# Norm statistics turned around: squares as the loaded operand, a token per partition, broadcast with the unit matrix

## The chip, the cores and the metric

The kernel runs on one core of a Trainium2 chip. The metric is the device time of one execution in microseconds; lower is better. All arithmetic of the norms is float32.

## The reference

One inference step of a small diffusion backbone with two layers (width D = 1024). Two token sets go through the same weights: 128 context tokens and 512 latent tokens. Layer 0 mixes tokens with a bidirectional state-space scan (four groups of 512 channels), layer 1 with differential attention (8 heads of 128 channels); each is followed by a gated convolutional FFN with 2816 hidden channels. What matters here are the root mean square norms:

```python
def _rms(x):
    xf = x.astype(F32)
    return xf * lax.rsqrt(jnp.mean(xf * xf, axis=-1, keepdims=True) + EPS)

y = _rms(y.reshape(b, l, SSD_GROUPS, SSD_INNER // SSD_GROUPS))   # per scan group, 512 channels
o = (_rms(o) * subln_g * (1.0 - lam_init))                       # per attention head, 128 channels
h = rmsnorm(x, g) * (1 + scale) + shift                          # before every mixer and FFN, 1024 channels
```

There are four norms over the model width inside the layers, one per scan group, one per attention head, and a final one over the model width.

## The kernel before

**Layout.** Activations lie transposed: channels on the 128 partitions, tokens along the free axis. The 512 latent tokens come first, then the 128 context tokens, 640 columns in all (`T`). A tensor of 1024 channels is 8 tiles of 128x640. The dense matmuls split weights and activations into a high and a low part of a reduced float32 format and make three products; each product is issued in two pieces, 256 columns (half A) and 384 columns (half B). For the last norm the tokens are cut the other way, 384 (half C) and 256 (half D). Weights stream in on SyncE's DMA queue, are rounded by ScalarE (`whi`) and VectorE (`wlo`), and are used once.

**A norm** sums over channels, so over partitions, which is done by matmul. `rms_bcast` (line 180) does it for all norms:

- `ms`: a 128x32 block of ones is the loaded operand (`lhsT`), the squares are streamed. The tokens are cut in four equal parts of n = 64, 96 or 160 columns; part j goes to the output partitions 32j to 32j+31. So the sums lie on a [128, n] tile, each of them 32 times over. If there are several tiles of squares (four for the norms inside and behind the layers: three of single channel tiles and one with the sum of five; eight for the very first norm), they accumulate in PSUM.
- `rsqrt` (line 165): an integer first guess and two refinements on VectorE, nine operations on [128, n] (tiles `rs_v`, `rs_a`, `rs_y`).
- The generator then yields, which lets other work be issued for `wait` steps.
- broadcast: a column of `sel` (0.375 at one of the partitions 0, 32, 64, 96, zero elsewhere), repeated to 128 columns, is the loaded operand, and `rs_y` is streamed. Each of four matmuls gives n columns, the same in all partitions. The tiles are called `nbc` (norms over the width), `gbc` (scan groups) and `obc` (heads). The factor 0.375 belongs to the last refinement.

Then VectorE multiplies the activations by the broadcast (`nt`, `xf`, `o`, `yt`).

`rms_bcast` runs 21 times: once for the first norm (all 640 tokens, eight tiles of squares, line 433), four times for the scan groups (640 tokens, one tile, line 832), eight times for the heads (640 tokens, one tile, line 1070), three times each for halves A and B of the norms between the sub-layers, and once each for C and D of the final norm (`norm_stats`, line 223).

**Order of the work.** The side work (scan, attention core, norms, modulation) is written as Python generators, kept in a list of tasks. Every dense k step calls `hook` (line 75), which counts a tick and advances the tasks whose wait is over; a task that yields w is taken up again w ticks later. One k step of a whole dense tile is six matmuls (three products, two halves); in the split last projections (`project_last`) and first tiles (`start_tiles`) it is three or six. From the program order a scheduler of the framework makes the queues of the engines; in the trace, for example, matmuls of a dense tile stand between those of one `ms`. Each engine works through its queue in order. Buffers that are reused (the PSUM tiles `d`, three in number, and `m` and `y`, one each, among others) are waited for.

Places where a norm's result is needed soon: after `project_last` the statistics of half A are computed while the last tiles' half B is still multiplied, and those of half B while the next sub-layer's first tiles (`st`) multiply half A. In `first_tiles` (line 366) the statistics stand ahead of the modulation rows (`modrow`), whose inputs (`mp`) come in by DMA into buffers that they free. At the end of the kernel, the statistics of half D, the root, the broadcast and the output tiles `yt` come after the last matmul of the last projection.

Of the kernel before, what the change touches and what calls it, by code (L numbers as in the profile page):

```python
# [18 lines left out]
P = 128  # L19
# [26 lines left out]
class Step:  # L46
# [118 lines left out]
    def rsqrt(self, y, ms, n, count):  # L165

        tile_ = lambda nm: self.pc.tile([P, 160], F32, tag=nm, name=nm, bufs=1)[:, :n]
        v, a = tile_("rs_v"), tile_("rs_a")
        V = self.nc.vector
        V.tensor_scalar(v, ms, 1.0 / count, EPS, ALU.mult, ALU.add)  # L170
        V.tensor_scalar(y.bitcast(I32), v.bitcast(I32), -0.5, RSQRT_MAGIC, ALU.mult, ALU.add)
        self.stt(a, y, -0.5, y, ALU.mult, ALU.mult)
        self.tt(a, a, v, ALU.mult)
        self.stt(y, a, 1.5, y, ALU.add, ALU.mult)
        self.tt(a, v, y, ALU.mult)
        self.tt(a, a, y, ALU.mult)
        self.stt(a, a, -10.0 / 3, a, ALU.add, ALU.mult)
        self.stt(y, a, 5.0, y, ALU.add, ALU.mult)

    def rms_bcast(self, alloc, sq, t0, t1, count, wait=4):  # L180


        n = (t1 - t0) // 4
        ms = self.bank("m", "ms")
        for i, s in enumerate(sq):
            for j in range(4):
                self.mm(ms[32 * j:32 * j + 32, :n], self.ones, s[:, t0 + j * n:t0 + (j + 1) * n],
                        i == 0, i == len(sq) - 1)
        y = self.pc.tile([P, 160], F32, tag="rs_y", name="rs_y", bufs=2)[:, :n]
# [3 lines left out]
        for j in range(4):  # L193
            self.mm(bc[:, j * n:(j + 1) * n], self.sel[:, j:j + 1].to_broadcast([P, P]), y, True, True)
        return bc

    def wide(self, name):

        return self.dense_ps(name)[:, 192:192 + T]
# [23 lines left out]
    def norm_stats(self, half):  # L223

        tag = {"A": "y", "B": "m", "C": "y", "D": "m"}[half]
        return self.rms_bcast(lambda: self.bank(tag, "nbc"), self.nsq, *HALF[half], D, 3)
# [78 lines left out]
    def load_consts(self):  # L305
        nc, a = self.nc, self.a
        self.ident, self.U, self.L = (self.cst[:, i * P:(i + 1) * P] for i in range(3))
        self.ones = self.cst[:, 3 * P:3 * P + 32]
        self.sel = self.cst[:, 3 * P + 32:3 * P + 36]
# [56 lines left out]
    def first_tiles(self, h, pool):  # L366
# [6 lines left out]
        self.cst = self.ct([P, 3 * P + 36], "cst")  # L373
# [656 lines left out]
    def att_tail(self, hd, w, ws, vs, os_, pool):  # L1030
# [39 lines left out]
        bc = yield from self.rms_bcast(lambda: self.wide("obc"), [sq], 0, T, P, 4 if hd == 7 else 7)  # L1070
# [114 lines left out]
def _consts():  # L1185
# [5 lines left out]
    cst = np.concatenate([I, U, L, np.ones((P, 32), f), f(0.375) * I[:, ::32]], axis=1)  # L1191
# [85 lines left out]
```

## Time and profile before

| | us |
|---|---|
| median of 3 runs | 1921.22 |
| lowest, highest | 1920.97, 1921.40 |
| the profiled execution | 1921.78 |
| its span, first to last instruction | 1920.0 |
| busy in it: TensorE, VectorE, ScalarE | 1887.8, 1377.3, 944.5 |

How to read the profile's lines. PE is TensorE's matmul, PEld its weight load (it overlaps PE), DVE is VectorE, ACT ScalarE, SP SyncE's DMA queue. In a timeline, a line gives the start in us from the start of the span, the duration in us, the engine, the line of the code, the operation and `out<-in` by tile names; "128*32 128x160 f32" is a matmul with 128 rows and 32 columns of the array in use and 128 partitions x 160 columns streamed. "x8" at the end are eight such instructions merged; in brackets stands the idle time before and what ended it. A matmul's duration includes its way through the array, so consecutive ones overlap: the distance between their starts, not the duration, is what one costs. In a view of one tile, three numbers with slashes are the least, median and greatest duration in ns, then come the first and last start. In the table by stretches each engine has its busy us and its count, and the last three columns are the granted TensorE clock, the DMA engines' share and GB/s. A line of the waits has the us in total, how often, and the longest.

### The profile page before, as it was taken

Reading aid. Unit: us, or ns where it says so; the run is one execution under the profiler, and the core shown is the slowest. Engines: PE = TensorE matmul, PEld = TensorE weight load, DVE = VectorE, ACT = ScalarE, POOL = GpSimd, SP = SyncE. Lnnn points to the kernel's source line nnn. Section 1 sums busy time; section 2 is a strip of 40 time slices with the busy share of each in tenths; the row PEclk is TensorE's granted clock in tenths of the full one; section 3 lists DMA queues with packets and bytes.
Section 4 is the critical chain, followed back from the end, with each engine's and each line's share of the span. In section 5 each row is a group of like instructions: output and inputs, shape, how many; then the busy total and the mean of one; then the engine's idle time right before and its main releaser. Section 6 shows DMA issues by size and latency. Waiting matters only on the chain.

```text
span 1920.0 us, 33586 instructions
## 1 busy us (share of the span) xinstructions
PE 1887.8 (98%) x13741; PEld 1781.4 (93%) x13741; DVE 1377.3 (72%) x2649; ACT 944.5 (49%) x1753; POOL 0.2 (0%) x4
## 2 busy tenths in 40 slices
PE   7999999999999999999999999999999999999997
PEld 4899898989989999999999989888899999999997
DVE  4779998989847999994455877788677553553554
ACT  3468585858525542343343566666446432441441
POOL 0000000000000000000000000000000000000000
PEclk9999999999999999999999999999999999999998
DMA  9612112123452556642222211111032222222211
GB/s 341 230 56 67 56 55 78 45 67 101 158 173 78 181 181 206 208 138 75 77 68 76 86 38 50 49 46 34 13 121 80 77 77 78 65 68 88 72 40 55
DMA packets 66730, 185.01 MB, mean 96 GB/s; under 512 B 8336, under 2 KB 14736, under 8 KB 66448
## 3 DMA queue, kind: packets, MB, share of 16 engines
q1 hardware_dynamic: 66000, 182.34, 29.3%
q8 instruction: 108, 1.77, 0.4%
q10 hardware_dynamic: 576, 0.52, 0.1%
q14 instruction: 46, 0.38, 0.1%
HBM read 177.06 MB, written 5.77 MB: 95 GB/s over the span
## 4 chain that ended last, share of the span: by engine, by line
PE 94%; DVE 2%; DMA 1%; ACT 1%; issue 0%; SPq 0%; DVEq 0%; ACTq 0%
PE up L103 30%; PE po L103 25%; PE z L103 6%; PE x L103 5%; PE st L103 5%; PE bc L103 3%; PE yp L103 3%; PE v L103 3%; PE q L103 2%; PE sl L103 2%; PE k L103 2%; PE ov L103 1%; PE modrow L103 1%; PE r L103 1%; PE wt L1052 1%; PE in L103 1%
## 5 line engine op out<-in xcount | busy, mean ns | idle before, releaser
L94 ACT ACTIVATE whi<-raw 128x1024 fp32r<-128x1024 f32 (+4 forms) x230 | 236.0, 1027 | 414.4 <-PE po L103 243.7
L100 DVE TENSOR_TENSOR wlo<-raw,whi 128x1024 fp32r<-128x1024 f32 (+4 forms) x230 | 270.3, 1177 | 183.8 <-ACT whi L94 178.1
L97 DVE SCALAR_TENSOR_TENSOR xr<-po,mod,xr 128x256 f32<-128x256 f32 (+2 forms) x231 | 89.0, 434 | 159.0 <-PE po L103 158.8
L103 PE MATMUL po<-mh,whi 128*128 128x256 f32 (+1 forms) x704 | 167.5, 310 | 0.0
L103 PE MATMUL po<-ml,whi 128*128 128x256 f32 (+1 forms) x704 | 167.2, 309 | 0.0
L103 PE MATMUL po<-mh,wlo 128*128 128x256 f32 (+1 forms) x704 | 167.0, 309 | 0.0
L103 PE MATMUL up<-h01h,wlo 128*128 128x256 f32 (+1 forms) x656 | 149.4, 308 | 0.0
L103 PE MATMUL up<-h11h,wlo 128*128 128x256 f32 (+1 forms) x656 | 149.4, 308 | 0.0
L103 PE MATMUL up<-h01h,whi 128*128 128x256 f32 (+1 forms) x656 | 149.3, 308 | 0.0
L103 PE MATMUL up<-h11h,whi 128*128 128x256 f32 (+1 forms) x656 | 149.3, 308 | 0.0
L103 PE MATMUL up<-h01l,whi 128*128 128x256 f32 (+1 forms) x656 | 149.3, 308 | 0.0
L103 PE MATMUL up<-h11l,whi 128*128 128x256 f32 (+1 forms) x656 | 149.3, 308 | 0.0
L103 PEld LDWEIGHTS po<-mh,whi 128*128 128x128 f32 x704 | 128.3, 188 | 0.6 <-ACT mh L94 0.4
L103 PEld LDWEIGHTS po<-mh,wlo 128*128 128x128 f32 x704 | 128.6, 188 | 0.0
L103 PEld LDWEIGHTS po<-ml,whi 128*128 128x128 f32 x704 | 128.4, 188 | 0.0
L103 PEld LDWEIGHTS up<-h01h,wlo 128*128 128x128 f32 x656 | 119.3, 188 | 0.0
L103 PEld LDWEIGHTS up<-h11h,wlo 128*128 128x128 f32 x656 | 119.3, 188 | 0.0
L103 PEld LDWEIGHTS up<-h11h,whi 128*128 128x128 f32 x656 | 119.3, 188 | 0.0
L103 PEld LDWEIGHTS up<-h01h,whi 128*128 128x128 f32 x656 | 119.3, 188 | 0.0
L103 PEld LDWEIGHTS up<-h01l,whi 128*128 128x128 f32 x656 | 119.3, 188 | 0.0
L103 PEld LDWEIGHTS up<-h11l,whi 128*128 128x128 f32 x656 | 119.2, 188 | 0.0
L97 DVE SCALAR_TENSOR_TENSOR ca<-uraw,fcw,ca 128x511 f32<-128x511 f32 (+1 forms) x176 | 85.2, 546 | 11.7 <-ACT ca L94 11.7
(505 smaller groups left out, 4469.2 us busy)
## 6 DMA issues: line engine op xcount, KB each, us to landing
raw<-in_w_up SPq DMA_DIRECT2D x88, 512.0 KB, 3.5
mw<-in_modT SPq DMA_DIRECT2D x48, 512.0 KB, 3.6
raw<-in_w_in SPq DMA_DIRECT2D x40, 512.0 KB, 3.5
raw<-in_w_dn SPq DMA_DIRECT2D x32, 448.0 KB, 3.3
raw<-in_w_qkv SPq DMA_DIRECT2D x24, 512.0 KB, 3.5
mr<-in_mod SPq DMA_DIRECT2D x44, 256.0 KB, 5.4
raw<-in_w_so SPq DMA_DIRECT2D x16, 512.0 KB, 4.1
raw<-in_w_dn SPq DMA_DIRECT2D x16, 512.0 KB, 3.7
```

What stands on the lines that cost most here:

```text
L94: return self.nc.scalar.activation(out, in_, func, **k)
L97: return self.nc.vector.scalar_tensor_tensor(out, in0, s, in1, op0, op1)
L100: return self.nc.vector.tensor_tensor(out, a, b, op)
L103: return self.nc.tensor.matmul(out, lhsT, rhs, start=start, stop=stop)
L1052: nc.tensor.transpose(pm[:, b * P:(b + 1) * P], ws[b][:, kc * P:(kc + 1) * P], self.ident)
```

## The change

The roles of the operands in the statistics are exchanged. Each 128 tokens of a tile of squares (128 channels x 128 tokens) become the loaded operand, and one column of ones is streamed. The sum of a token lands on the token's own partition, in column j for the j-th 128 tokens, so `ms` is [128, 2], [128, 3] or [128, 5] instead of [128, 64], [128, 96] or [128, 160]. The first matmul of a norm alone has the start flag, the last alone the stop flag. The root runs on these few columns and has a tenth operation, the multiplication by 3/8 that was in the selectors before. The broadcast loads column j of the root, repeated to 128 columns, and streams the unit matrix: the result has in every partition the roots of 128 tokens, and there is one such matmul for every 128 tokens. The waits between the statistics and the broadcast are shorter: 3 ticks instead of 4 as a rule, 2 instead of 3 for halves A to D, 5 instead of 7 for the heads (3 instead of 4 for the last head). The wide broadcast tile begins at column 128 of its two PSUM banks instead of 192, so that no chunk of 128 crosses a bank. The constants lose 31 columns of ones and the four selectors.

```diff
     def rsqrt(self, y, ms, n, count):
-        tile_ = lambda nm: self.pc.tile([P, 160], F32, tag=nm, name=nm, bufs=1)[:, :n]
+        tile_ = lambda nm: self.pc.tile([P, NCH], F32, tag=nm, name=nm, bufs=1)[:, :n]
...
         self.stt(y, a, 5.0, y, ALU.add, ALU.mult)
+        V.tensor_scalar(y, y, 3.0 / 8, None, ALU.mult)
...
-    def rms_bcast(self, alloc, sq, t0, t1, count, wait=4):
-        n = (t1 - t0) // 4
+    def rms_bcast(self, alloc, sq, t0, t1, count, wait=3):
+        n = (t1 - t0) // P
         ms = self.bank("m", "ms")
         for i, s in enumerate(sq):
-            for j in range(4):
-                self.mm(ms[32 * j:32 * j + 32, :n], self.ones, s[:, t0 + j * n:t0 + (j + 1) * n],
-                        i == 0, i == len(sq) - 1)
-        y = self.pc.tile([P, 160], F32, tag="rs_y", name="rs_y", bufs=2)[:, :n]
+            for j in range(n):
+                self.mm(ms[:, j:j + 1], s[:, t0 + j * P:t0 + (j + 1) * P], self.ones, i + j == 0, i + j == len(sq) + n - 2)
+        y = self.pc.tile([P, NCH], F32, tag="rs_y", name="rs_y", bufs=2)[:, :n]
         self.rsqrt(y, ms[:, :n], n, count)
         yield wait
         bc = alloc()
-        for j in range(4):
-            self.mm(bc[:, j * n:(j + 1) * n], self.sel[:, j:j + 1].to_broadcast([P, P]), y, True, True)
+        for j in range(n):
+            self.mm(bc[:, j * P:(j + 1) * P], y[:, j:j + 1].to_broadcast([P, P]), self.ident, True, True)
         return bc
     def wide(self, name):
-        return self.dense_ps(name)[:, 192:192 + T]
+        return self.dense_ps(name)[:, P:P + T]
...
-        return self.rms_bcast(lambda: self.bank(tag, "nbc"), self.nsq, *HALF[half], D, 3)
+        return self.rms_bcast(lambda: self.bank(tag, "nbc"), self.nsq, *HALF[half], D, 2)
...
-        self.ones = self.cst[:, 3 * P:3 * P + 32]
-        self.sel = self.cst[:, 3 * P + 32:3 * P + 36]
+        self.ones = self.cst[:, 3 * P:3 * P + 1]
...
-        self.cst = self.ct([P, 3 * P + 36], "cst")
+        self.cst = self.ct([P, 3 * P + 1], "cst")
...
-        bc = yield from self.rms_bcast(lambda: self.wide("obc"), [sq], 0, T, P, 4 if hd == 7 else 7)
+        bc = yield from self.rms_bcast(lambda: self.wide("obc"), [sq], 0, T, P, 3 if hd == 7 else 5)
...
-    cst = np.concatenate([I, U, L, np.ones((P, 32), f), f(0.375) * I[:, ::32]], axis=1)
+    cst = np.concatenate([I, U, L, np.ones((P, 1), f)], axis=1)
```

## The prediction

> **What bounds the kernel now.** I read the page first, then the waits, then the order of time around each norm. The page's head and its PE lines, and the line of the chain that ended last:
>
> ```profile
> span 1920.0 us, 33586 instructions
> ...
> PE 1887.8 (98%) x13741; PEld 1781.4 (93%) x13741; DVE 1377.3 (72%) x2649; ACT 944.5 (49%) x1753; POOL 0.2 (0%) x4
> ...
> PE 94%; DVE 2%; DMA 1%; ACT 1%; issue 0%; SPq 0%; DVEq 0%; ACTq 0%
> ...
> raw<-in_w_in SPq DMA_DIRECT2D x40, 512.0 KB, 3.5
> ```
>
> TensorE sets the end (the last line, a transfer's size and time to landing, is for the start). The table by stretches says the same of four attention heads, where VectorE and ScalarE have room:
>
> ```profile
> 1176.00:1322.00 146.00, 146.00 (x1026) 131.31 (x1028) 114.24 (x228) 89.76 (x190) 0.00 (x0) 1.00 0.15 46
> ```
>
> So a microsecond added to PE's queue between some 50 and 1903 us is a microsecond of the end, and one taken from VectorE there is worth next to nothing. The change is therefore a question of PE slots: what the statistics and the broadcast take of PE now, and after.
>
> **What one load costs.** The program has two PE instructions, each with its own weight load, for one float32 matmul (8 where the code asks for 4). The loads of the broadcasts, in the order of time: eight that stream 64 columns, eight that stream 96 and the load behind them; then their row in the view of one tile (ns, least/median/most):
>
> ```profile
> 585.32 0.97 PEld L103 LDWEIGHTS nbc<-rs_y,cst 128*128 128x128 f32 x8 [0.24 <-DVE rs_y L97]
> ...
> 601.91 0.97 PEld L103 LDWEIGHTS nbc<-rs_y,cst 128*128 128x128 f32 x8
> 602.80 0.19 PEld L103 LDWEIGHTS st<-h01l,whi 128*128 128x128 f32 x1
> ```
> ```profile
> L103 PEld LDWEIGHTS nbc<-rs_y,cst x72: 185/190/338, 16.9 to 1909.2; 128*128 128x128 f32 x72
> ```
>
> Both groups of eight loads last 0.97 us: the streamed width does not matter, the load does. From 601.91 to 602.80 are eight loads, 0.89 / 8 = 0.111 us each. That is the price of a full 128x128 float32 weight tile when little is streamed through it, and after the change every statistic matmul is of this kind: 128 columns of squares loaded, one column streamed. The trace has no one-column matmul, so 0.111 is carried over from 64 and 96 columns; a lower bound comes with the rivals.
>
> **The statistics now.** They load a 128x32 tile of ones and four of them share the array. Each block is priced by the slots it displaces: from the matmul before it to one behind it, less the ordinary pitches in between. One attention head (640 tokens, one tile of squares):
>
> ```profile
> 1175.48 0.45 PE L103 MATMUL q<-h10l,whi 128*128 128x256 f32 x2
> 1175.77 0.46 PE L103 MATMUL q<-h10h,wlo 128*128 128x256 f32 x2
> 1176.15 0.48 PE L103 MATMUL ms<-osq,cst 128*32 128x160 f32 x8
> ...
> 1176.96 0.46 PE L103 MATMUL q<-h10l,whi 128*128 128x256 f32 x2
> ```
>
> A pair takes 0.295 us; 1175.48 to 1176.96 is 1.48, less three pairs: 0.60 us, refill of the array included. After: 5 tiles of 128 tokens, 10 instructions, 1.11 us. So +0.51.
>
> Half A (256 tokens, four tiles of squares), half B (384 tokens) and the last norm's half C (384), in this order:
>
> ```profile
> 582.00 0.34 PE L103 MATMUL po<-y10h,wlo 128*128 128x384 f32 x1
> 582.27 0.32 PE L103 MATMUL ms<-nsq,cst 128*32 128x64 f32 x8
> 582.40 0.52 PE L103 MATMUL ms<-sq,cst 128*32 128x64 f32 x24
> ...
> 583.13 0.33 PE L103 MATMUL po<-y11l,whi 128*128 128x384 f32 x1
> 583.30 0.34 PE L103 MATMUL po<-y11h,wlo 128*128 128x384 f32 x1
> ...
> 595.95 0.28 PE L103 MATMUL st<-h01h,wlo 128*128 128x256 f32 x1
> ...
> 597.80 0.37 PE L103 MATMUL ms<-sq,cst 128*32 128x96 f32 x8
> ...
> 598.33 0.28 PE L103 MATMUL st<-h01h,wlo 128*128 128x256 f32 x1
> ...
> 1895.32 0.28 PE L103 MATMUL po<-mh,wlo 128*128 128x256 f32 x1
> ...
> 1895.72 0.68 PE L103 MATMUL ms<-sq,cst 128*32 128x96 f32 x24
> ...
> 1896.55 0.28 PE L103 MATMUL po<-ml,whi 128*128 128x256 f32 x1
> ```
>
> A: 1.13 less two pitches of 0.175 = 0.78 us now; after, 4 tiles x 2 chunks x 2 = 16 loads, 1.78. B: 2.38 less six pitches of 0.12 = 1.66 now (it is cut in three and pays the refill three times); after, 24 loads, 2.66. C: 1.23 less two pitches = 0.99; after 2.66. Each grows by 1.0 to 1.7 us.
>
> **The broadcast.** On 640 tokens now, with the last step of the root before it:
>
> ```profile
> 1181.70 0.30 DVE L97 SCALAR_TENSOR_TENSOR rs_y<-rs_a,rs_y 128x160 f32<-128x160 f32 x1
> ...
> 1187.42 0.46 PE L103 MATMUL k<-h10h,whi 128*128 128x256 f32 x2
> ...
> 1187.83 1.25 PE L103 MATMUL obc<-rs_y,cst 128*128 128x160 f32 x8
> ...
> 1189.09 0.45 PE L103 MATMUL k<-h10h,wlo 128*128 128x256 f32 x2
> ```
>
> 1.67 less two pairs = 1.08 us; after, 10 instructions of 128 columns at the load's 0.111: 1.11, +0.03. For 256 tokens eight loads become four (-0.44), for 384 six (-0.22). This is the only part in which PE wins. The root was ready at 1182.0 and used at 1187.83, so the shorter waits (two steps of a dense tile sooner in the heads, one elsewhere) find it ready. It also claims one of the three wide PSUM buffers sooner; if that one's reader is late, PE stands there, which the range's upper end holds.
>
> **The root on VectorE.** Nine operations on 64 to 160 columns become ten on 2 to 5. Two small dependent operations of a softmax are 0.20 us apart:
>
> ```profile
> 1140.29 0.17 DVE L997 RECIPROCAL sm<-sm 128x2 f32<-128x2 f32 x1 [1.00 <-ACT e L94]
> 1140.49 0.16 DVE L100 TENSOR_TENSOR sm<-sm,nlam 128x1 f32<-128x1 f32 x1
> ```
>
> Ten are 2.0 us. That saves a microsecond of VectorE on 640 tokens, but PE works on other tiles meanwhile. It counts only where PE stands and waits for the root: at the end, and in one wait at the attention's start that the table of waits shows:
>
> ```profile
> PE nbc L103 <- DVE nlam L100: 0.9, 1, 0.9
> ```
>
> There PE is 0.9 us too early for VectorE, and the longer statistics of half B would fill up to that; I take half, -0.4.
>
> **The end.** Statistics, root, broadcast and the first output stand in series:
>
> ```profile
> 1903.89 0.32 PE L103 MATMUL ms<-nsq,cst 128*32 128x64 f32 x8
> ...
> 1905.11 0.32 PE L103 MATMUL ms<-sq,cst 128*32 128x64 f32 x8 [0.68 <-ACT sq L94]
> 1905.50 0.23 DVE L170 TENSOR_SCALAR rs_v<-ms 128x64 f32<-128x64 f32 x1 [0.89 <-PE ms L103]
> ...
> 1907.88 1.60 PEld L103 LDWEIGHTS nbc<-rs_y,cst 128*128 128x128 f32 x8 [2.61 <-issue]
> ...
> 1909.71 7.42 DVE L97 SCALAR_TENSOR_TENSOR yt<-xr,gains,nbc 128x256 f32<-128x256 f32 x16 [1.95 <-PE nbc L103]
> ```
>
> After: twelve loads from 1903.89 fill the wait for the last square (to 1905.22), the last four end at 1905.67 instead of 1905.43: +0.24. From 1905.50 to the broadcast's loads are 2.38, 0.12 of it handover; the root of 2.0 instead of 2.26: -0.26. Eight broadcast loads take (1.60-0.19)/7 = 0.20 each here; four go: -0.80. Net -0.8.
>
> **The start.** Here PE is the slower by half and waits for data. The first statistics (view of the tile, first 20 us), two equal groups of another tile a little later, and the transfer in the chain that ended last:
>
> ```profile
> L103 PE MATMUL ms<-sq,cst x64: 472/474/476, 6.1 to 12.8; 128*32 128x160 f32 x64
> ...
> 18.25 0.66 PE L103 MATMUL modrow<-mp,s 128*32 128x128 f32 x8
> ...
> 20.80 0.39 PE L103 MATMUL modrow<-mp,s 128*32 128x128 f32 x8
> ...
> 21.95 5.35 DMA mp<-in_modp
> ```
>
> Eight modrow instructions shrink from 0.66 to 0.39 us between 18 and 21, so until then the array ran at about half rate, though the clock column there says 1.00. Now 64 instructions follow the squares one by one and end at 13.3. After: 80 loads, 8.9 us at 0.111 (end near 15) or 17.8 at twice that (near 24). Behind them in PE's queue stand the modulation rows, which free the buffers for the next weights. What covers the delay is the backlog of that transfer: 5.35 us against the page's median of 3.5, 1.9, and the shorter root: nine steps of 0.30 with their gaps, 3.1, against 2.0, 1.1. So 0 to +7.7. I take +2: with PE working without a gap from 6 us, the full rate should come after the first few squares rather than after 20 us.
> By the Trainium skill (TensorE: Matmul & The Clock Gate, What's actually happening) the clock opens after some 3.4 us of sustained work; that would put the end of the statistics near 17 and the cost near 1, if loads with one streamed column count as work, which no run here shows.
>
> The constants shrink by 35 columns and the broadcast's bank offset moves: nothing.
>
> **The sum.** Heads and groups: 12 x (0.51 + 0.03) = 6.5. A: 3 x (1.00 - 0.44) = 1.7. B: 3 x (1.00 - 0.22) = 2.3. C: 1.67 - 0.22 = 1.45. Together 12.0 on PE; start +2, wait -0.4, end -0.8: **+12.8 us**. The profiled execution took 1921.78 us (1.78 around its span) and stands 0.56 above the median: 1921.78 + 12.8 - 0.56 = **1934.0 us**, 0.7% slower.
>
> **Rivals.**
> *The loads hide and the streamed columns alone count: faster.* For: four-way packing shows as little as 0.024 us an instruction (0.78 / 32 in half A). Against: the 0.97 us that 64 and 96 columns share. At 0.024, heads and groups are 12 x (0.24 - 0.60 + 0.03) = -4.0, A 3 x (0.38 - 0.78 - 0.44) = -2.5, B 3 x (0.58 - 1.66 - 0.22) = -3.9, C -0.6, end -1: -12, **1909**. It wins as soon as a load costs less than about 0.06.
> The Trainium skill (TensorEngine Tiling (Array Packing), Instruction Overhead) says that a matmul of one streamed column costs as much as one of 60 cycles, 25 ns at 2.4 GHz: alone it gives this rival's time. The same skill (TensorE: Matmul & The Clock Gate, LDWEIGHTS) puts a load at columns / 1.2 ns, 107 for 128; the trace's 0.111 agrees with that one.
>
> *The clock drops.* At 1907.88 a load costs 0.20 after PE stood 2.6 us. If 2.7 us of one-column matmuls (B, C) look like standing still, the matmuls behind them run at half rate for some microseconds: four places at 2 us, and the start at its upper end (+5.7 more): **1948**. Against: the loads themselves never pause.
>
> *PE's growth falls into waits: no change.* Then only the start and the end remain, **1922**. For: VectorE is 1 us lighter per head, the roots come sooner. Against: 1176 to 1322 has no idle PE to fill.
>
> **Chances.** Forecast 0.76, clock 0.08, hidden loads 0.09, swallowed 0.07. Range **1926 to 1944**: below, 0.09 us a load (264 more loads in the sum, -5.5) and a free start; above, the start's upper end and 4 us of badly placed waits. What differs by under 0.2% (3.8 us) from before a measurement can't tell from no change. Faster 0.10, same 0.08, slower 0.82.
>
> **What would show it.** Right: full-width loads of ms 0.11 us apart, some 1.1 us per head and 2.7 in B and C; the waits of PE no larger; the yt group about 0.8 us sooner after the last po. Wrong: ms instructions under 0.06 us apart (first rival), the matmuls behind them above 0.175 us apart or modrow slow beyond 21 us (second), PE idle between 100 and 1890 us (a wait that I did not price).

## The result, and the profile after

The changed kernel takes **1949.27 us** (median of 4 executions, 1943.56 to 1949.98); the kernel before took 1921.10 beside it. The ratio is 1.0141, with a 95% interval of 1.0121 to 1.016. Forecast were 1934.0 and 1926 to 1944: the direction was right, the size less than half of it. Executions of one kernel differ among themselves by some us, so below medians are set against medians, and a trace against the time of its own execution.

The profiled execution is the shortest of the four, 1943.56. Its page:

```profile
span 1941.8 us, 33501 instructions
...
PE 1911.5 (98%) x13687; PEld 1819.3 (94%) x13687; DVE 1360.6 (70%) x2670; ACT 944.3 (49%) x1753; POOL 0.2 (0%) x4
...
PE 95%; DVE 2%; ACT 2%; DMA 0%; issue 0%; SPq 0%; DVEq 0%; ACTq 0%
```

VectorE lost 17 us of work and PE gained 24; PE still sets the end. Where the time came from can be read by following one dense matmul (counted in program order, so it is the same work) through both traces. The table gives by how much it falls further behind before in each stretch between two such marks, and the forecast's terms for the same stretch. The column "again" is a second profile of the same changed kernel, in an execution of 1948.14 us; the last two are experiments below.

| stretch of before (us) | what lies in it | forecast | after | again | 96 columns | 96 columns, groups wait 4 |
|---|---|---|---|---|---|---|
| 0 to 112 | first norm | +2.0 | +8.54 | +7.70 | +0.54 | +1.37 |
| 112 to 462 | three groups | +1.63 | +1.63 | +1.48 | +1.61 | +1.74 |
| 462 to 605 | fourth group, A, B | +1.88 | +4.70 | +8.14 | +3.79 | +1.80 |
| 605 to 1081 | A, B, wait for nlam | +0.94 | +0.85 | +0.36 | +1.30 | +0.74 |
| 1081 to 1460 | eight heads, A, B | +5.66 | +5.70 | +5.75 | +6.45 | +6.44 |
| 1460 to the end | C, end | +0.65 | +0.37 | +2.92 | +1.35 | +0.74 |
| sum | | +12.8 | +21.8 | +26.4 | +15.0 | +12.8 |

Two rows are far off, the first and the third. The first has a scatter of its own: in the six kernels below that compute the first norm as before it lies between -1.29 and +1.36. The median adds a third miss: the three executions without a profile are another 5.4 to 6.4 us longer than the profiled one.

**The first norm.** From the chain that ended last in after, the pieces from 6 to 37 us, and the same stretch of both kernels in the table by stretches (last three columns: clock, DMA share, GB/s):

```profile
6.34 17.24 PE ms L103 x80
...
26.11 0.80 PE nbc L103 x2
...
36.74 7.02 PE in L103 x36
```
```profile
24.00:32.00 8.00, 5.63 (x71) 3.82 (x67) 1.85 (x9) 1.05 (x3) 0.00 (x0) 1.00 0.49 161
```
```profile
24.00:32.00 8.00, 6.60 (x73) 4.49 (x74) 6.33 (x14) 2.19 (x5) 0.00 (x0) 0.79 1.05 386
```

The 80 loads take 17.24 us, 0.215 each, to the very last. The modulation rows stand behind them, their buffers come free late, and the transfers run dry: DMA share 0.49 in after (first of the two rows) against 1.05 in before. The first dense matmul (`in`) starts at 36.74 instead of 28.9.

**One head.** Timeline of after, statistics, first and last step of the root, and the broadcast:

```profile
1193.15 0.46 PE L103 MATMUL q<-h10h,wlo 128*128 128x256 f32 x2
...
1193.44 1.17 PE L103 MATMUL ms<-cst,osq 128*128 128x1 f32 x10
1194.65 0.17 DVE L170 TENSOR_SCALAR rs_v<-ms 128x5 f32<-128x5 f32 x1 [1.44 <-PE ms L103]
...
1194.85 0.46 PE L103 MATMUL q<-h10l,whi 128*128 128x256 f32 x2
...
1196.47 0.17 DVE L179 TENSOR_SCALAR rs_y<-rs_y 128x5 f32<-128x5 f32 x1
...
1201.52 1.19 PEld L103 LDWEIGHTS obc<-cst,rs_y 128*128 128x128 f32 x10 [0.28 <-ACT e L94]
```

From the pair of the dense matmul ahead of the statistics to 1194.85 are 1.70 us; two pairs of 0.295 lie in it (one is left out above), which leaves 1.11, as forecast. The root is ten steps 0.20 apart, 1.99 us with the last one's duration. The broadcast's ten loads take 1.19, 0.119 each, but it stands 0.28 first, until an exponential (`e`) has left the score buffer that it wants: the wait that the forecast had put into its upper end.

**The end** became shorter, as forecast (a little more):

```profile
1926.73 0.50 PE L103 MATMUL ms<-cst,nsq 128*128 128x1 f32 x4
...
1930.75 0.52 PEld L103 LDWEIGHTS nbc<-cst,rs_y 128*128 128x128 f32 x4 [2.18 <-issue]
...
1931.50 7.42 DVE L97 SCALAR_TENSOR_TENSOR yt<-xr,gains,nbc 128x256 f32<-128x256 f32 x16 [0.87 <-PE nbc L103]
```

From the first statistics of half D to the first output tile are 4.77 us; in before 1903.89 to 1909.71, 5.82. That is -1.05, forecast were -0.8.

### The profile page after: what moved, and what is told of

The parts are those of the page before. It is cut to its first block, busy times and chain, and to the rows that moved or that the text cites. A ratio compares the mean times of both kernels' runs of the same rounds, so it can differ in the third digit from the quotient of the medians.

```text
span 1941.8 us, 33501 instructions
## 1 busy us (share of the span) xinstructions
PE 1911.5 (98%) x13687; PEld 1819.3 (94%) x13687; DVE 1360.6 (70%) x2670; ACT 944.3 (49%) x1753; POOL 0.2 (0%) x4
## 3 DMA queue, kind: packets, MB, share of 16 engines
q1 hardware_dynamic: 66000, 182.32, 28.9%
## 4 chain that ended last, share of the span: by engine, by line
PE 95%; DVE 2%; ACT 2%; DMA 0%; issue 0%; SPq 0%; DVEq 0%; ACTq 0%
PE up L103 30%; PE po L103 25%; PE z L103 6%; PE x L103 5%; PE st L103 5%; PE bc L103 3%; PE yp L103 3%; PE v L103 3%; PE q L103 2%; PE ms L103 2%; PE sl L103 2%; PE k L103 2%; PE ov L103 1%; PE in L103 1%; PE modrow L103 1%; PE wt L1051 1%
```

## The experiments

All kernels compute the whole reference; where squares are rounded, that is said. Medians are of 4 to 12 executions, the kernel before beside them at 1921.06 to 1921.77. Where a part is computed as before, the old functions stand beside the new ones as `rms_bcast_old`, `rsqrt_old` and `wide_old`.

**First round: is it the start, or the shorter waits?** The changed kernel once more, unedited:

> The changed kernel once more, unaltered, for a second trace. Its first profiled execution took 1943.6 us, its three others 1949.0 to 1950.0, so about 6 us are still without a place. Theory 1 (clock at the start): the first norm's one-column matmuls leave the array at half rate, and how long that lasts differs from execution to execution; a trace of 1949 us then differs from the first one before 60 us and nowhere else, by about 6 us. Rival: the array's clock also drops behind the one-column blocks of the later norms (580 to 620, 1070 to 1090, 1440 to 1465, 1917 to 1925 us) in some executions; the 6 us then lie there.

Then the first norm by the old code:

```diff
-        st = self.rms_bcast(lambda: self.wide("nbc"), sq, 0, T, D)
+        st = self.rms_bcast_old(lambda: self.wide_old("nbc"), sq, 0, T, D)
```

> The first norm alone goes back to the old code (ones loaded, squares streamed, root on 160 columns, selectors); all 20 other norms stay changed. In the trace of the changed kernel the dense tiles of the first projection begin 8.55 us later than before, and the end is 21.8 us later. Theory 1: those 8.55 us come from the 80 half-rate loads of the first norm and go away, so the span is about 1933.3 us; if the 6 us between executions also sit at the start, the times are all near 1935 and no longer differ by 6 us. Rival: the start's loss would have been absorbed by waits later, so the time falls by less than 4 us; or the 6 us stay, and executions at 1935 and 1941 both occur.

The first norm by the new code, with 96 columns of ones streamed; the loads and their number stay, the root reads every 96th column of the sums:

```diff
-                self.mm(ms[:, j:j + 1], s[:, t0 + j * P:t0 + (j + 1) * P], self.ones, ...)
+                self.mm(ms[:, c * j:c * j + c], s[:, t0 + j * P:t0 + (j + 1) * P], self.ones96 if c > 1 else self.ones, ...)
...
-        self.rsqrt(y, ms[:, :n], n, count)
+        self.rsqrt(y, ms[:, :c * n:c], n, count)
...
-        st = self.rms_bcast(lambda: self.wide("nbc"), sq, 0, T, D)
+        st = self.rms_bcast(lambda: self.wide("nbc"), sq, 0, T, D, c=96)
```

> As the changed kernel, but in the first norm alone 96 columns of ones are streamed behind each load instead of one; the number of loads (80) and their width stay. Theory 1a (the clock opens on streamed work): the array leaves the half rate within the first norm, loads go from 0.215 to 0.11 us apart, the norm's block ends some 5 us or more sooner than at 23.6 us, and the start's loss shrinks from 8.5 to about 2 to 4 us, as I forecast. Theory 1b (the rate at the start has nothing to do with what is streamed): the loads stay 0.215 us apart to the end of the block and the time stays at 1943 to 1950 us. If streaming itself costs, the loads become slower than 0.215 us and the time rises.

And the waits of before with everything else changed:

```diff
-    def rms_bcast(self, alloc, sq, t0, t1, count, wait=3):
+    def rms_bcast(self, alloc, sq, t0, t1, count, wait=4):
...
-        return self.rms_bcast(lambda: self.bank(tag, "nbc"), self.nsq, *HALF[half], D, 2)
+        return self.rms_bcast(lambda: self.bank(tag, "nbc"), self.nsq, *HALF[half], D, 3)
...
-        bc = yield from self.rms_bcast(lambda: self.wide("obc"), [sq], 0, T, P, 3 if hd == 7 else 5)
+        bc = yield from self.rms_bcast(lambda: self.wide("obc"), [sq], 0, T, P, 4 if hd == 7 else 7)
```

> As the changed kernel, but with the waits of before (4, 3, 7, and 4 in the last head). In the changed kernel's trace each of the middle heads takes 37.47 us instead of 36.45, 0.5 more than the price of loads explains, and the broadcast stands 0.18 us for a PSUM buffer (the wait ends with ACT e). Theory 2: asking for the wide buffer two steps sooner costs that 0.2 to 0.5 us per head; with the old waits a middle head takes about 37.0 us and the time falls by 2 to 4 us. Rival: the head's growth is all loads and refills; the heads stay at 37.5 us and the time within 1 us of the changed kernel's own.

| | median (range) | ratio, 95% |
|---|---|---|
| changed kernel again | 1948.95 (1944.15 to 1950.37) | 1.0135, 1.0117 to 1.0152 |
| first norm old | 1942.98 (1939.33 to 1946.24) | 1.0107, 1.009 to 1.0125 |
| first norm 96 columns | 1940.09 (1937.65 to 1943.84) | 1.0095, 1.0076 to 1.0113 |
| waits old | 1947.62 (1945.21 to 1952.51) | 1.0141, 1.0122 to 1.016 |

The start is settled. With the old first norm the matmul at 112 us is 1.3 us earlier than in before and not 8.5 later. The time fell by 6.3 us only, though, to 1942.98 and not to the expected 1935: this trace loses 7.9 us between 462 and 605 us, where the clock is at one half from 603.3 to 610.1, and 2.9 from 1871 us to the end. With 96 columns the matmul is 2.0 later, and the view of one tile's instructions by stretches shows why (us, PE busy and count, clock, DMA share, GB/s), first the kernel with 96 columns, then after:

```profile
5.90:10.30 4.40, 4.35 (x20) 1.00 1.02 396
10.30:17.20 6.90, 6.90 (x62) 1.00 1.07 386
```
```profile
6.30:10.70 4.40, 4.36 (x21) 1.00 1.01 378
10.70:17.60 6.90, 6.90 (x34) 1.00 1.05 383
17.60:23.50 5.90, 5.90 (x28) 1.00 1.03 394
```

With 96 columns the loads go at 0.21 us for 4.4 us and then at 0.11 (62 in 6.90 us); with one column they stay at 0.21 to the end. So PE's clock rises after some microseconds of float32 loads with 96 streamed columns and doesn't rise within 17 us behind loads that stream one, though these never pause. The clock column says 1.00 throughout; here the distances say more. The clock records kept in the traces agree: none of them reaches back before a first change to full clock, and that change stands at 10.5 us here and at 30.2 us in after.

The waits are not the main cost: with the old ones the time is 1.3 us shorter than the repeat's (expected were 2 to 4, with a middle head of 37.0 us; it takes 37.8). Between 462 and 605 us the kernel with the old waits loses 2.4 instead of 4.7, and between 1081 and 1460 more, 8.5 us against 5.7. The first six heads are not the reason: up to 1345 us it loses 5.5 there, after 7.3. From 1345 to 1390 it loses another 1.6, while after gains 3.0 back. In that place before's trace has a stretch at half clock, the old waits' trace has one too (1383.9 to 1390.7), and neither trace of after has one. The table by stretches of before, then of the kernel with 8 columns from the fourth round, which has the waits of after and such a stretch, and gains back only 0.5:

```profile
1365.40:1372.20 6.80, 6.80 (x34) 5.70 (x35) 5.29 (x15) 2.60 (x5) 0.00 (x0) 0.50 0.11 31
```
```profile
1387.50:1394.20 6.70, 6.70 (x30) 6.35 (x31) 4.85 (x16) 1.69 (x4) 0.00 (x0) 0.50 0.07 22
```

So this stretch is worth some 2.5 us (an estimate, 3.0 less 0.5), nearly all of the difference between 8.5 and 5.7, and it comes with the new waits too. Why the fourth group is dearer with 3 ticks is in the chain that ended last, after first, then the kernel with 96 columns and 4 ticks from the next round:

```profile
522.53 1.12 PE modrow L103 x8
...
523.96 5.03 DMA mr<-in_mod
...
529.04 1.05 PE modrow L103 x2
530.08 1.31 PE gbc L103 x10
```
```profile
517.24 1.09 PE ms L103 x10
518.33 2.67 PE po L103 x18
521.00 1.11 PE gbc L103 x10
522.11 16.73 PE po L103 x114
```

In after the modulation rows of the second set come up in PE's queue before their transfer has landed, and the group's broadcast stands behind them. The waits of the weight loads from 515 to 560 us (us in total, times, longest) have the sum; PE itself stands 0.75 us of it:

```profile
PEld modrow L103 <- DMA mr<-in_mod: 2.2, 3, 1.7
```
With the old wait the rows come later and the transfer is in no chain. How long the transfer takes differs from execution to execution. In the second profile of the changed kernel, timeline of PE:

```profile
529.84 1.40 PE L103 MATMUL modrow<-mr,s 128*32 128x512 f32 x2 [2.54 <-DMA mr<-in_mod]
531.17 2.50 PE L103 MATMUL gbc<-cst,rs_y 128*128 128x128 f32 x10
```

PE stands 2.54 us, and behind that the clock is at one half from 530.4 to 533.8, in which the broadcast takes 2.50 instead of 1.38 us. That is how this row comes to 8.14 instead of 4.70.

**A clue in these traces.** The records of the clock have stretches of one half directly behind statistics with one column. Half C in the changed kernel's second profile, timeline and table by stretches:

```profile
1921.60 0.72 PE L103 MATMUL ms<-cst,sq 128*128 128x1 f32 x6
...
1922.85 0.28 PE L103 MATMUL po<-mh,whi 128*128 128x256 f32 x1
1922.97 0.35 PE L103 MATMUL po<-ml,whi 128*128 128x256 f32 x1
...
1923.33 0.42 PE L103 MATMUL po<-mh,whi 128*128 128x256 f32 x1
1923.55 0.41 PE L103 MATMUL po<-ml,whi 128*128 128x256 f32 x1
```
```profile
1919.00:1923.00 4.00, 4.00 (x38) 4.00 (x37) 0.77 (x5) 0.52 (x1) 0.00 (x0) 1.00 0.00 0
1923.00:1926.40 3.40, 3.40 (x19) 3.40 (x18) 1.51 (x9) 0.42 (x1) 0.00 (x0) 0.51 0.00 0
```

Dense matmuls of 256 columns go from 0.12 us apart to 0.21 for 3.4 us, while PE is busy all the time. The next round was made to test this.

**Second round: parts alone, and wide columns everywhere.** Only the groups and heads new, and only the halves new (in both, the first norm goes by the old functions as in the first round's diff):

```diff
-        return self.rms_bcast(lambda: self.bank(tag, "nbc"), self.nsq, *HALF[half], D, 2)
+        return self.rms_bcast_old(lambda: self.bank(tag, "nbc"), self.nsq, *HALF[half], D, 3)
```

> Only the twelve norms of one tile (four scan groups, eight heads) are as in the changed kernel, with its shorter waits; the first norm and halves A to D are computed as before. Theory 1 (only the price of a load counts, 0.111 us each): 12 x 0.54 = +6.5 us over before, 1927.7. Theory 2 (the shorter waits put the broadcast and its neighbours in worse places): the period of a head grew by 1.04 us in the changed kernel's trace and the stretch of the fourth scan group by some 2.6 us over its terms, so 8 x 1.04 + 4 x 0.54 + 2.6 = +13, about 1934. The clock theory expects nothing here, because a block of ten one-column loads lasts 1.1 us: no row below full clock beyond those of before.

```diff
-        bc = yield from self.rms_bcast(lambda: self.wide("gbc"), [sq], 0, T, 512)
+        bc = yield from self.rms_bcast_old(lambda: self.wide_old("gbc"), [sq], 0, T, 512)
...
-        bc = yield from self.rms_bcast(lambda: self.wide("obc"), [sq], 0, T, P, 3 if hd == 7 else 5)
+        bc = yield from self.rms_bcast_old(lambda: self.wide_old("obc"), [sq], 0, T, P, 4 if hd == 7 else 7)
```

> Only halves A, B, C and D are as in the changed kernel, with their shorter wait; first norm, groups and heads are computed as before. Price theory: 1.7 + 2.3 + 1.45 - 0.4 - 0.8 = +4.3 us, 1925.5, executions within 1 us of each other. Clock theory (2.7 us of one-column loads look like a pause to the clock): drops to half the clock for 3.4 or 6.8 us right behind the blocks of B and C in the trace, in some executions at B and in most at C, 1.5 to 3.5 us each: 1927 to 1932, the executions several us apart.

The 96 columns as the default for all norms, and the same with the groups' old wait:

```diff
-    def rms_bcast(self, alloc, sq, t0, t1, count, wait=3):
+    def rms_bcast(self, alloc, sq, t0, t1, count, wait=3, c=96):
```

> All statistics stream 96 columns of ones in place of one, the root reads every 96th column; loads, waits and everything else as in the changed kernel. 96 columns should take no longer than one beside a load of 0.11 us. Clock theory: no clock row below 0.9 behind B or C any more, the first norm costs about 2 us as in the kernel in which it alone was widened, executions within 2 us of each other, about 1937. If the drops behind B and C have another cause than the single column: 1940 to 1944 as in that kernel, drops at the same places.

```diff
-        bc = yield from self.rms_bcast(lambda: self.wide("gbc"), [sq], 0, T, 512)
+        bc = yield from self.rms_bcast(lambda: self.wide("gbc"), [sq], 0, T, 512, 4)
```

> As the kernel with 96 columns everywhere, but the scan groups wait 4 ticks between root and broadcast, as before the change, and not 3. If the shorter wait of group 3 brings the next modulation rows' loads too close (the 5 us transfer in the chain of waits), this is 2 to 2.5 us faster than the kernel with 96 columns and 3 ticks, about 1935, and PE does not wait for the modulation rows' transfer near 525 us. If the longer statistics cause it and not the wait, the two are within 0.5 us.

| | median (range) | ratio, 95% |
|---|---|---|
| groups and heads only | 1933.96 (1928.34 to 1935.99) | 1.0063, 1.0041 to 1.0085 |
| halves only | 1928.72 (1923.43 to 1930.49) | 1.0034, 1.0016 to 1.0051 |
| 96 columns everywhere | 1936.41 (1935.91 to 1936.81) | 1.008, 1.0064 to 1.0096 |
| the same, groups wait 4 | 1934.63 (1932.64 to 1934.8) | 1.0068, 1.0048 to 1.0087 |

Streaming 96 columns where one is enough makes the kernel 12.9 us **faster** than the changed one (1949.27 to 1936.41; the intervals of the ratios don't touch), and its four executions lie within 0.9 us of each other. 8.0 of it are the start (8.54 to 0.54 in the table above; over all rounds the start costs 6.2 to 8.5 us with 1, 8 or 32 columns and 0.5 to 2.0 with 96 in float32). The rest can't be read from the first profile of after, which had no drop behind B or C. The second profile shows where a longer execution of this kernel loses its time: of the 4.6 us by which its trace is longer, 3.4 lie at the fourth group (the longer transfer and the half clock behind that wait) and 2.6 from C to the end (the drop shown above); the other rows give 1.4 back. So it was not theory 1, by which the start alone would differ. That the executions without a profile lose theirs in the same two places is likely; their mean clocks, 0.991 and 0.992 against 0.996, fit. Counted over all rounds, eight profiled executions have few columns in the halves (1, 8 or 32): six of them have a half-clock stretch behind C, and two behind a half B. Of the seven with 96 columns there none has one behind its statistics; but three of these seven load once instead of twice and so have shorter blocks, which leaves four to compare with. With the drop, the stretch from 1871 us to the end grows by 2.3 to 2.9 us; without it by 0.4 and 1.2 with few columns, and by 0.7 to 1.9 in the four with 96. The row of the halves-only kernel, then of 96 columns everywhere at the same place of its C:

```profile
1901.90:1905.30 3.40, 3.40 (x17) 3.40 (x17) 1.87 (x11) 0.00 (x0) 0.00 (x0) 0.50 0.00 0
```
```profile
1909.70:1912.30 2.60, 2.60 (x26) 2.60 (x25) 0.00 (x0) 0.35 (x1) 0.00 (x0) 1.00 0.00 0
1912.30:1914.70 2.40, 2.28 (x20) 2.08 (x18) 1.84 (x12) 0.00 (x0) 0.00 (x0) 1.00 0.00 0
```

The groups' old wait gives 1.8 us (expected 2 to 2.5); in the traces it is 2.0 between 462 and 605 us. And this kernel, in which the clock's drops behind the statistics and the transfer are out of the way, stands at **1934.63**, 12.8 us over before in its trace: the forecast's sum. That agreement is luck in part: its trace lacks the half-clock stretch that before's has at 1365 us.

Of the parts, the halves took 1928.72, within the 1927 to 1932 that the clock's drops were expected to give, with the drop behind C. Groups and heads agree with both expectations, and so with neither: the trace is 6.6 us over before's, as by the price of the loads (1927.7), the median 12.9 over, as by badly placed waits (1934). Why its executions spread over 7.6 us stays open: the profiled one has no half-clock stretch that before's lacks, and one that took 1934.59 has a mean clock of 0.995, against 0.996 in the shortest. The transfer at the fourth group, for which PE's loads wait 0.9 us in this trace and 3.7 in the longest, may be a part of it; no run shows that.

**Third round: does the number of loads set the price?** Squares and ones are rounded to the reduced float32 format of the dense matmuls; one instruction and one load then do the work of two. Based on the kernel with 96 columns and 4 ticks:

```diff
-        sq = self.slot("sq", "osq", bufs=1)
+        sq = self.slot("sq", "osq", F32R, bufs=1)
...
-                self.mm(..., self.ones96 if c > 1 else self.ones, ...)
+                self.mm(..., self.ones_r, ...)
```

(and so for the other tiles of squares)

> As the kernel with 96 columns everywhere and 4 ticks for the groups, but squares and ones are rounded to the reduced float32 format of the dense matmuls, for which one instruction and one load do the work of two; everything else the same. The sums lose some low bits by it. Price theory (the number of full loads sets the cost, 0.111 us each): outside the first norm 12 x 5 + 3 x 8 + 3 x 12 + 12 = 132 loads fewer, -14.7 us, and up to 1 us at the first norm and the last: 1934.6 - 15 = 1919 to 1921, so level with before. Rival (what costs is something per norm, refill and handover, not per load): less than 5 us gained, above 1929.

The parts alone again, with the column of ones repeated to 96 by its address pattern:

```diff
-                self.mm(ms[:, j:j + 1], s[:, t0 + j * P:t0 + (j + 1) * P], self.ones, ...)
+                self.mm(ms[:, c * j:c * j + c], s[:, t0 + j * P:t0 + (j + 1) * P], self.ones.to_broadcast([P, c]), ...)
```

> Only the twelve norms of one tile as in the changed kernel, with a column of ones repeated to 96 columns; first norm and halves as before. The same with one column had a profiled execution 6.6 us over before's and others up to 8 us longer than that. If the clock reacts to blocks of 1.1 us of one-column loads too: executions within 2 us of each other, 1928 to 1930. If that spread is of another kind: again 1928 to 1936 with a median near 1934.

> Only halves A to D as in the changed kernel, with a column of ones repeated to 96 columns. Clock theory: no clock row behind C, the 2.4 us that appeared between 1871 and the end in the one-column form shrink to 1 or less, executions within 2 us of each other, near 1921.1 + 4.3 = 1925.4. Otherwise 1928.7 as in the one-column form.

And a mixture that could have beaten both kernels, the halves in the reduced format and all else as before:

> A mixture: first norm, groups and heads as before; halves A to D with squares loaded, the column of ones repeated to 96, both in the reduced float32 format, one load in place of two. Price theory: A 8 x 0.111 = 0.89 - 0.78 - 0.44 = -0.33, B 1.33 - 1.66 - 0.22 = -0.55, three times each -2.6; C 1.33 + 0.1 - 0.99 - 0.22 = +0.2; the end -1: about -3.4 us, 1917.7, faster than both kernels. Rival (the wait of the attention's start and the work around the halves take it back): 1920 to 1922.

| | median (range) | ratio, 95% |
|---|---|---|
| one load in place of two | 1928.54 (1926.24 to 1932.03) | 1.004, 1.0026 to 1.0054 |
| groups and heads, 96 columns | 1929.36 (1927.38 to 1931.45) | 1.0039, 1.0024 to 1.0054 |
| halves, 96 columns | 1927.02 (1926.27 to 1928.13) | 1.0026, 1.0016 to 1.0036 |
| halves, one load for two | 1922.02 (1918.09 to 1929.65) | 1.0007, 0.9996 to 1.0018 |

Neither theory held: 6 us gained where 14 to 15 or less than 5 were expected. The two parts with 96 columns came out at 1929.36, within 4.1 us (expected 1928 to 1930, within 2), and at 1927.02, within 1.9 us and without a drop behind C, but between the expected 1925.4 and 1928.7. The stretches say where one load for two helps. In the three groups the growth of 1.74 us disappears wholly (-0.06): there the loads set the price. In the heads hardly anything is gained although the block of statistics shrinks (growth from 1140 to 1345 us 5.8, with two loads 5.9). Heads are periodic, so the first and the last `ms` of four heads measure it (view of one tile: least, median, greatest ns, first and last start). Before; after; 96 columns with 4 ticks; one load for two:

```profile
L103 PE MATMUL ms<-osq,cst x32: 299/311/323, 1176.2 to 1285.7; 128*32 128x160 f32 x32
```
```profile
L103 PE MATMUL ms<-cst,osq x40: 166/250/250, 1193.4 to 1306.8; 128*128 128x1 f32 x40
```
```profile
L103 PE MATMUL ms<-cst,osq x40: 245/275/275, 1185.2 to 1298.0; 128*128 128x96 f32 x40
```
```profile
L103 PE MATMUL ms<-ones_r,osq x20: 207/274/275, 1180.1 to 1292.3; 128*128 128x96 f32 x20
...
1187.52 1.19 PEld L103 LDWEIGHTS obc<-cst,rs_y 128*128 128x128 f32 x10 [0.76 <-ACT e L94]
```

Less the length of the last block (0.35, 1.0, 1.0 and 0.45 us) and divided by three, a head takes 36.4, 37.5, 37.3 and 37.25 us. Half of the loads are gone in the last one, and the period is the same: what PE saves at `ms` it stands at the broadcast (last row, 0.76 until an exponential has emptied the buffer) and at the score tiles (`sl`).

This kernel also bounds what was said of the columns. Its first norm streams 96 columns too, one load of the reduced format in place of two. Timeline of PE:

```profile
8.03 7.70 PE L103 MATMUL ms<-ones_r,sq 128*128 128x96 f32 x35 [0.87 <-DVE sq L100]
```

These 35 loads go without a pause at 0.22 us each, half rate to the last, where the float32 loads with 96 columns went to 0.11 after 4.4 us. The first record of full clock stands at 20.7 us. So it is not the number of streamed columns alone that opens the clock; the format counts too.

In the mixture the halves give back their gain in the same way. Timeline of its first half B:

```profile
597.11 0.83 PE L103 MATMUL ms<-ones_r,sq 128*128 128x96 f32 x6
...
598.61 0.53 PE L103 MATMUL ms<-ones_r,sq 128*128 128x96 f32 x3 [0.37 <-ACT sq L94]
...
601.89 0.91 PE L103 MATMUL nbc<-cst,rs_y 128*128 128x128 f32 x6 [0.23 <-DVE rs_y L179]
```

PE now waits for the last square and for the root, which the longer statistics had covered. The mixture is level with before; nothing here beats it.

**Fourth round: the heads' wait, and how many columns the clock needs.** The old waits (first round's diff) with 96 columns; the old heads' wait with one load for two; and 8 and 32 columns in place of 96:

> 96 columns of ones everywhere and the waits of before (4 ticks as a rule, 3 for the halves, 7 and 4 for the heads), the rest as in the changed kernel. If the shorter waits are what costs beyond the price of the loads (2.0 us at the fourth group, about 0.4 us in each head, where the broadcast now claims its buffer before a pair of score tiles does): 1936.4 - 2.0 - 3 = 1931 to 1932, and a head's period of 37.0 us or less. If the heads' growth is something else: 1934.6 as with the groups' wait alone, or slower, and a period of 37.3 us or more.

> As the kernel with one reduced-format load in place of two, but the heads wait 7 and 4 ticks as before the change and not 5 and 3. There the statistics of a head take 0.67 us, as before the change (0.68), and the head's period still is 37.25 us and not 36.45; its broadcast stands 0.65 us for its buffer. If the wait of 5 ticks is the reason: period 36.5 us and 1928.5 - 6 = 1922.5, level with before. If not: within 2 us of 1928.5.

```diff
-    def rms_bcast(self, alloc, sq, t0, t1, count, wait=3, c=96):
+    def rms_bcast(self, alloc, sq, t0, t1, count, wait=3, c=8):
```

> As the kernel with 96 columns of ones everywhere (waits of the changed kernel), but 8 columns. If any small stream that is not one column keeps the clock: 1936.4, the 80 loads of the first norm done by 17.5 us. If the clock goes by the time for which columns stream, 8 columns are hardly more than one: 1947 to 1949, the 80 loads at 0.215 us to about 23.5 us, and clock rows of 0.5 behind B or C.

> As before, with 32 columns. 32 columns of one pass take 13 ns at the full clock beside a load of 111 ns. If the clock goes by the share of time in which columns stream, this lies between: 1937 to 1949, the first norm's loads turning fast later than with 96 columns (where the last ones end at 17.2 us) and earlier than 23.5 us.

| | median (range) | ratio, 95% |
|---|---|---|
| 96 columns, waits old | 1934.4 (1931.88 to 1935.75) | 1.0061, 1.0046 to 1.0076 |
| one load for two, heads wait 7 | 1929.12 (1927.51 to 1930.03) | 1.0035, 1.0022 to 1.0048 |
| 8 columns | 1946.73 (1943.11 to 1948.05) | 1.0121, 1.0104 to 1.0138 |
| 32 columns | 1949.2 (1946.23 to 1953.62) | 1.0142, 1.0121 to 1.0162 |

Waiting 7 ticks again doesn't bring a head's 36.4 us back. Both kernels have 37.05, with two loads and with one (expected were 37.0 or 37.3 for the first, 36.5 or the same time as with 5 ticks for the second):

```profile
L103 PE MATMUL ms<-cst,osq x40: 245/275/275, 1183.1 to 1295.3; 128*128 128x96 f32 x40
```
```profile
L103 PE MATMUL ms<-ones_r,osq x20: 207/274/275, 1181.2 to 1292.8; 128*128 128x96 f32 x20
```

So neither loads nor ticks alone set it. The ticks are not without effect, though: from 1140 to 1345 us the growth falls from 5.9 to 3.8 with two loads and from 5.8 to 3.6 with one. The medians show little of it. The broadcast again stands for an exponential; in the timeline VectorE's small root steps now lie among its other work (before, a pair's two reductions of the scores followed each other; here one pair's second starts 0.7 us after the first ended, behind a weighted sum). That gap alone doesn't explain it: with 5 ticks the pairs follow each other and a head takes 37.25. No run changed the order of VectorE's work alone, so this part stays open.

In float32, 8 and 32 columns behave as one. In the first norm the view of the tile by stretches with 32 columns gives

```profile
6.30:10.70 4.40, 4.40 (x22) 1.00 0.98 364
10.70:17.60 6.90, 6.90 (x34) 1.00 1.04 364
17.60:23.50 5.90, 5.34 (x26) 1.00 1.00 386
```

which is half rate to the end, as with one. So in float32 the point from which a stream opens the clock lies between 32 and 96 columns for a load of 0.11 us; in the reduced format 96 were not enough in 7.7 us.

## Why the prediction was wrong, point by point

- **The start (+2): the step that failed.** It measured +8.5. The forecast's bound of 7.7 came from exactly this case, 80 loads at twice 0.111 to about 24 us; they ended at 23.6. I left it with the sentence that at work without a gap the full rate "should come after the first few squares". Work without a gap isn't enough: with the same 80 float32 loads, one streamed column left the array at half rate to the end and 96 brought the full rate, with a cost of 0.5 to 2.0 us. The condition that I had quoted beside it, "if loads with one streamed column count as work", was the whole question, and they don't. The Trainium skill (TensorE: Matmul & The Clock Gate, What's actually happening) speaks of sustained work of some 3.4 us; with 96 float32 columns the rate rises after 4.4 to 6.4 us, with 1 to 32 columns 17 us were not sustained work.
- **The second rival (clock drops, 1948 us, 0.08) named the time almost exactly**, and my argument against it, that the loads themselves never pause, fell with the same observation. That it came so close is luck in part. The start's share is 6.5 us over the forecast (5.7 said), but drops behind C come in six of eight traces and behind B in two, 1 to 3 us each, not 2 at all four places in every execution, and the transfer at the fourth group, 2.8 us and more, was not in it.
- **The fourth group (+0.54 became about +3):** the shorter wait was taken as free, "the shorter waits find it ready". It was free for the root, but it let the group's broadcast and the next modulation rows meet, 2.2 us of PE's loads waiting for a transfer (3.7 in the second profile). I had named late PSUM readers as the risk of an earlier broadcast, not a DMA further back in the queue. The old wait gives 1.8 us back.
- **The price of a load, 0.111 us: right.** 0.111 with the clock up (62 in 6.90 us); 1.11 us per head; the three groups grew by 1.63 as forecast and by nothing once the loads were halved. The first rival (streams alone count, 1909) falls with it. Halves A and B (1.34 a pair) measured 1.4 in the kernel with 96 columns and 4 ticks, but they are not only PE's price: with half the loads PE waits for squares and root.
- **The heads (8 x 0.54): right in the sum by luck.** The stretch with the heads grew by 5.70 for a forecast of 5.66, but a middle head grew by 1.04 and not by 0.54. Up to 1345 us, six heads, the growth was 7.3; from 1345 to 1390 us 3.0 came back, some 2.5 of it because before's trace has a half-clock stretch there and after's has none. Halving the loads changed next to nothing. I had said that the heads have no idle PE to fill; saved loads do turn into waits there, as the third rival said, but the added ones cost more than their price.
- **C and the end:** -1.05 for -0.8 at the end, +1.4 to +1.5 for C (forecast +1.45) in the first profile of after, where no drop follows: right there. The other traces without a drop and with two loads have 1.8 for C.

Added up for the median: 12.8 forecast, +6.5 at the start and +2.8 around the fourth group make 22, the first trace's 21.8; measured are 28.2. The rest is the 5 to 6 us by which most executions are longer than the first profile. The second profile has 4.6 of them, in the transfer's longer wait with the half clock behind it and in the drop behind C; for the executions without a trace the same causes are likely and not shown.

## What to carry to other kernels

A matmul that loads a full float32 tile to stream one column was priced here by its load (0.11 us), and it also looked idle to TensorE's clock: the chain of 80 at the start ran at half rate, and the matmuls behind a block of under 3 us did in six traces of eight. Streaming 96 columns of the same ones cured both (0.11 us a load either way); in the reduced format 96 didn't open the clock at the start. The other way is to keep the ones stationary. When a wait is shortened, look past the result that it waits for to what else comes up in the queue at that moment, transfers above all; and where a ring of buffers sets the pace, count neither a saved nor an added load of TensorE as time until a run has shown it.

## What was not expected of the hardware

- Float32 loads back to back for 17 us, with one, 8 or 32 streamed columns, leave the array at 0.214 us a load; 96 columns bring 0.111 after 4.4 to 6.4 us. In the reduced format, with one load for two, 96 columns leave it at 0.22 for 7.7 us. The profile's clock column shows 1.00 in all these cases for the first 20 us.
- Some 2 to 2.7 us of matmuls with 1 or 8 streamed columns can put the following dense matmuls at half rate for 3.4 or 6.8 us, with PE busy in every moment. It doesn't happen in every execution. Of the changed kernel's spread of 6 us it is one part in the second profile (2.6 of 4.6 us), the transfer and the half clock behind a wait of 2.5 us the other. Before too spread over 8 us in one round (1918.74 to 1926.9 in 21).
